# Recurrent branch, memory attention and pool product emitted one step behind every fifth dense product

## The chip, the cores and the metric

The kernel runs on one core of one Trainium2 chip. The metric is the device time of one execution in microseconds, the median of three runs. The engines are TensorE (PE in the profile, its weight loads PEld), VectorE (DVE), ScalarE (ACT), GpSimd (POOL) and SyncE (SP, which here issues the DMAs).

## The reference

One layer of a streaming encoder on 2048 tokens of width 1024, all float32, cut to what matters:

```python
h = rms_norm(x, norm_mix_g)
p = h @ w_in_mix                                  # 1792 rwkv + 256 pool + 256 memory query columns
y_a = rwkv7_branch(p_rwkv, ...)                   # 8 heads of 64, delta rule:
#   s_kk = S @ kk_t
#   S = S * w_t - outer(s_kk, kk_t * a_t) + outer(v_t, k_t);  y_t = S @ r_t
#   then group norm per head, bonus sum(r*k*r_k)*v, output gate
y_b = pool_branch(p_pool, pool_w, pool_scale)     # causal means over 2/4/8/16 tokens, 64x64 products
y_c = memory_branch(q_mem, rms_norm(mem), w_mem_kv)   # 4 heads, softmax over 256 memory tokens
gates = sigmoid(h @ w_gate + b_gate)              # three gates of 1024
merged = gates[0] * (y_a @ w_up_rwkv) + gates[1] * (y_b @ w_up_pool) + gates[2] * (y_c @ w_up_mem)
x = x + merged @ w_o
x = x + conv_ffn(rms_norm(x), ...)                # 1024 -> 2 x 2816 -> 1024, depthwise conv of 3, GELU
out = rms_norm(x, norm_final_g)
```

## The kernel before

**Tiling.** The mixers run over four tiles of 512 tokens (`for i in range(NT)`, L868); the FFN follows in two halves of 1024 tokens. Channels lie on the partitions, tokens on the free axis.

**Dense products.** Every dense product is made in three passes of high and low parts: for each 128 rows of the contraction three matmuls of 512 columns, hi x hi, hi x lo, lo x hi (`dense_fm`, L165 to L167; `dense_acc`, L173 to L175). A weight piece is 128 x 512 as hi and lo, 512 KB, and serves twelve matmuls in the mixers. In the first tile a piece is loaded as float32 and split (hi on ScalarE, L131, lo on GpSimd, L132), and the result is written to a cache in DRAM; the later tiles load the pieces from there (`wsp<-wc_...`). The pieces go through a ring of `WB` = 4 buffers.

**The recurrent branch** takes the eight heads in four pairs (b = 0 to 3). Of each pair, `rkv(b)` projects r, k and v. `rwkv()` is the preparation: the lora products (L452, L453), a head sum (`head_sum`, L302 and L303, two matmuls with a matrix of ones), a prefix scan, the scaled keys `E` (in `Z`) and `BK`, their products chunk by chunk (L510) under masks (L516 to L519), a bounce of the strictly triangular blocks through DRAM (`Ld` to `As`), and a forward substitution in 62 short VectorE operations (L539 and L541 in turn, "the solve"), whose result `X` goes through DRAM (`Xd`) into the block diagonal `TB`. `rwkv_chain()` then centres v (L562, L563), transposes BK into `BKt` (L572), joins the blocks of the inverse (`T`, L576; L580, L587) and goes through eight chunks of 64 tokens in sequence. A chunk step is three links, each a TensorE product and a short operation that the next one needs: L600, then `Rn` (L602 on VectorE, L603 on ScalarE); L607, then `UV` (L608, L609); L610, then the state `SV` (L615). After the eighth chunk come the outputs Y (L621, L624), the group norm and the output gate.

**Memory attention** (`mem_branch`) forms scores (L291 to L293), a softmax, its transposes (L423) and the product with the values; **pool** (`pool_branch`) forms running means on GpSimd and VectorE and one product (L385).

**Order.** A string of tokens, `SEQ`, gives the order in which a tile's blocks are written: `aN` the projections of pair N, `rN` its preparation, `cN` its whole chain, `pN` pool, `qN` and `mN` memory queries and attention, `gN` a block of gates 1 and 2 and `vN` the pool and memory up-projections, `kN` a block of gate 0, and `l x e s` loads and norm sums. After the string come the recurrent up-projection and w_o. The scheduler of the tile framework may move instructions against the written order when its model finds an operand late, so the chain's links end up between dense products.

## Time and profile before

| | us |
|---|---|
| Time, median of 3 runs (lowest to highest) | 3464.53 (3462.49 to 3466.19) |
| Profiled execution, its own time | 3465.13 |
| its span | 3463.3 |
| TensorE busy | 3278.9 |
| VectorE busy | 1884.8 |
| ScalarE busy | 1073.2 |
| GpSimd busy | 920.3 |

The profile is one execution. Its span goes from the first to the last record. TensorE's matmuls are pipelined, and the ends of their records are modelled. In the rows that give busy times for a stretch, the columns are: start and end of the stretch in us, its length, busy time of PE, PEld, DVE, ACT and POOL (with the number of instructions), the mean granted TensorE clock as a share of full speed, the busy share of the DMA engines and GB/s. In rows on waits they are total us, number of waits and the longest; in rows on groups of instructions busy us and mean ns, then idle time before them. A float32 matmul of the side branches has two records, or a count of two.

The tiles' first lora products stand at 67.4, 599.9, 1064.7 and 1527.8 us, and the FFN begins at 1973 us; these are the cuts between the stages. Tile 2 is also cut at the first L600 of each pair's chain (1136.0, 1227.7, 1283.8, 1356.6) and at its eighth (1181.0, 1266.3, 1319.1, 1390.2).

### The profile page before, as it was taken

What the parts mean: (1) busy time and instruction counts of PE and PEld (TensorE: products, weight loads), DVE (VectorE), ACT (ScalarE), POOL (GpSimd) and SP (SyncE); (2) the same over time, 40 slices, a digit from 0 to 9 for tenths busy, and PEclk for the clock granted to TensorE, in tenths of its full rate; (3) what the DMA queues carried; (4) which work ended last, traced back from release to release, by engine and by line L of the source; (5) the groups of instructions that cost most, each with busy time, mean ns of one, the idle gap of its engine ahead of it and who ended that gap; (6) DMA issues with size and microseconds to landing.
All of it is one profiled execution on the core that took longest, in us unless ns stands there. A gap on an engine that the chain in (4) does not pass through costs nothing.

```text
span 3463.3 us, 44769 instructions
## 1 busy us (share of the span) xinstructions
PE 3278.9 (95%) x16752; PEld 2588.4 (75%) x16752; DVE 1884.8 (54%) x3610; ACT 1073.2 (31%) x1999; POOL 920.3 (27%) x1094
## 2 busy tenths in 40 slices
PE   6988899989999999999999999999999999999998
PEld 4765677666787667876677788888888778888887
DVE  4788641888437885348872433443445554344435
ACT  4354343434213432224342221221222322122122
POOL 4254443122111222021220232322322342232223
PEclk8999999999999999999999999999999999999999
DMA  7444677344574345663445721111112141111111
GB/s 242 156 159 153 206 257 248 117 131 137 169 248 152 119 122 167 222 190 107 139 141 164 261 61 40 61 46 38 59 51 67 49 155 46 37 58 53 37 49 64
DMA packets 203274, 431.18 MB, mean 124 GB/s; under 512 B 54193, under 2 KB 66097, under 8 KB 202929
## 3 DMA queue, kind: packets, MB, share of 16 engines
q1 hardware_dynamic: 203056, 428.32, 38.7%
q8 instruction: 132, 2.16, 0.3%
q14 instruction: 86, 0.70, 0.1%
HBM read 346.44 MB, written 81.80 MB: 124 GB/s over the span
## 4 chain that ended last, share of the span: by engine, by line
PE 71%; DVE 17%; DMA 4%; issue 3%; ACT 3%; POOL 1%; SPq 0%; POOLq 0%; ACTq 0%; DVEq 0%
PE mm L722 9%; PE mm L724 9%; PE mm L723 9%; PE mm L167 7%; PE mm L166 7%; PE mm L165 7%; DVE xm L539 4%; PE ch L759 4%; PE ch L757 4%; PE ch L758 4%; DVE X L541 3%; PE mx L510 1%; PE ch L600 1%; PE ch L607 1%; PE ch L610 1%
## 5 line engine op out<-in xcount | busy, mean ns | idle before, releaser
L132 POOL TENSOR_TENSOR wsp<-wraw,wsp 128x512 fp32r<-128x512 f32 x380 | 507.9, 1344 | 1123.3 <-ACT wsp L131 1080.6
L165 PE MATMUL mm<-h,wsp 128*128 128x512 f32 x1344 | 554.1, 413 | 7.5 <-ACT h L226 2.6
L167 PE MATMUL mm<-h,wsp 128*128 128x512 f32 x1344 | 555.6, 413 | 4.1 <-POOL wsp L132 3.8
L166 PE MATMUL mm<-h,wsp 128*128 128x512 f32 x1344 | 552.5, 411 | 0.6 <-POOL h L226 0.5
L131 ACT CAST wsp<-wraw 128x512 fp32r<-128x512 f32 x380 | 230.5, 618 | 819.5 <-PE mm L724 498.5
L165 PEld LDWEIGHTS mm<-h,wsp 128*128 128x128 f32 x1344 | 261.3, 194 | 60.6 <-issue 5.4
L167 PEld LDWEIGHTS mm<-h,wsp 128*128 128x128 f32 x1344 | 261.2, 194 | 57.9 <-POOL wsp L132 6.8
L761 DVE TENSOR_TENSOR acc<-acc,ch 128x512 f32<-128x512 f32 x288 | 197.9, 688 | 190.7 <-PE ch L759 189.1
L166 PEld LDWEIGHTS mm<-h,wsp 128*128 128x128 f32 x1344 | 261.4, 195 | 53.3 <-issue 3.1
L722 PE MATMUL mm<-h2a,wsp 128*128 128x512 f32 x704 | 276.7, 393 | 0.0
L722 PE MATMUL mm<-h2b,wsp 128*128 128x512 f32 x704 | 275.9, 392 | 0.0
L724 PE MATMUL mm<-h2a,wsp 128*128 128x512 f32 x704 | 275.5, 391 | 0.0
L724 PE MATMUL mm<-h2b,wsp 128*128 128x512 f32 x704 | 275.2, 391 | 0.0
L723 PE MATMUL mm<-h2b,wsp 128*128 128x512 f32 x704 | 274.3, 390 | 0.0
L723 PE MATMUL mm<-h2a,wsp 128*128 128x512 f32 x704 | 274.2, 389 | 0.0
L736 DVE TENSOR_SCALAR tg<-U,cwu 128x512 f32<-128x512 f32 x88 | 74.0, 841 | 294.4 <-ACT U L733 294.3
L539 DVE TENSOR_TENSOR xm<-X,As 128x16 f32<-128x16 f32 (+30 forms) x496 | 224.8, 453 | 12.4
L757 PE MATMUL ch<-G,wsp 128*128 128x512 f32 x576 | 226.8, 394 | 2.4 <-DVE acc L761 2.4
L759 PE MATMUL ch<-G,wsp 128*128 128x512 f32 x576 | 227.7, 395 | 0.0
L758 PE MATMUL ch<-G,wsp 128*128 128x512 f32 x576 | 226.7, 394 | 0.0
L606 POOL TENSOR_SCALAR SV<-SV,dC 64x64 f32<-64x64 f32 x224 | 120.9, 540 | 333.1 <-DVE SV L615 202.6
L747 DVE TENSOR_TENSOR G<-tg,G 128x512 fp32r<-128x512 f32 x88 | 89.9, 1021 | 122.4 <-ACT G L746 122.4
(350 smaller groups left out, 5879.5 us busy)
## 6 DMA issues: line engine op xcount, KB each, us to landing
wsp<-wc_w_gate SPq DMA_DIRECT2D x144, 512.0 KB, 3.7
wsp<-wc_w_in_mix SPq DMA_DIRECT2D x108, 512.0 KB, 3.4
wraw<-in_w_ffn_in SPq DMA_DIRECT2D x176, 256.0 KB, 2.7
wc_w_gate<-wsp SPq DMA_DIRECT2D x48, 512.0 KB, 3.0
wsp<-wc_w_o SPq DMA_DIRECT2D x48, 512.0 KB, 4.9
wraw<-in_w_ffn_out SPq DMA_DIRECT2D x88, 256.0 KB, 2.7
wc_w_in_mix<-wsp SPq DMA_DIRECT2D x36, 512.0 KB, 2.9
wraw<-in_w_gate SPq DMA_DIRECT2D x48, 256.0 KB, 3.8
```

The costliest lines, as they stand in the source:

```text
L131: sc.copy(hi, raw[:, :n])
L132: gp.tensor_tensor(lo, raw[:, :n], hi.bitcast(F32), ALU.subtract)
L165: te.matmul(acc, hi, act(0, k), start=k == 0, stop=False)
L166: te.matmul(acc, hi, act(1, k), start=False, stop=False)
L167: te.matmul(acc, lo, act(0, k), start=False, stop=k == kn - 1)
L539: ve.tensor_tensor(xm[:, :, 0:t + 1], X[:, :, 0:t + 1], As[:, 0:t + 1, t].unsqueeze(1).to_broadcast([P, 8, t + 1]), ALU.mult)
L722: te.matmul(ab[t], ws[j][0], hk(0, t, k), start=k == 0, stop=False)
L723: te.matmul(ab[t], ws[j][0], hk(1, t, k), start=False, stop=False)
L724: te.matmul(ab[t], ws[j][1], hk(0, t, k), start=False, stop=k == KB - 1)
L757: te.matmul(a, ws[j][0][:, cs], G[:, j, 0, tk], start=j == 0, stop=False)
L758: te.matmul(a, ws[j][0][:, cs], G[:, j, 1, tk], start=False, stop=False)
L759: te.matmul(a, ws[j][1][:, cs], G[:, j, 0, tk], start=False, stop=j == 1)
```

## The change

The tokens `a`, `r`, `c` and the second `m` leave the order string, and the ring of weight pieces shrinks from four buffers to three. `rwkv`, `rwkv_chain`, `mem_branch` and `pool_branch` become generators that yield at set places (`wait(n)` yields n times). All dense matmuls of the mixers go through `dense_mm`, which counts them, and behind every fifth (`SPACING`) calls `run()`, which moves each branch under way on by one step: attention, pool, the preparation of one pair and the chain of another. What a step writes is tied behind that matmul, and the scheduler does not move it ahead. A chain begins at the earliest 33 steps (`SOLVE`) after its pair's preparation has been written. A preparation that wants buffers of an older chain yields until that has read them (`free`). At a few places the remaining steps are run out at once (`until`). The BK transposes move from the chain to the preparation, `BKt` gets a second buffer, the stores to `Ld` move ahead of the bonus head sum, and some temporaries change buffers.

```diff
-WB = 4
+WB = 3
+SPACING, SOLVE = 5, 33
-SEQ = "a0 l x r0 e p0 p1 q0 m0 q1 a1 m1 c0 r1 a2 g0 r2 g1 v0 g2 g3 v1 g4 c1 a3 g5 v2 g6 c2 r3 g7 s v3 g8 g9 v4 g10 g11 v5 g12 g13 c3 v6 g14 g15 v7 k0 k1 k2 k3 k4 k5 k6 k7".split()
+ORDER = "l x e q0 q1 m p0 p1 g0 g1 v0 g2 g3 v1 g4 g5 v2 g6 g7 s v3 g8 g9 v4 g10 g11 v5 g12 g13 v6 g14 g15 v7 k0 k1 k2 k3 k4 k5 k6 k7".split()
+    def dense_mm(*args, **kw):
+        mm = te.matmul(*args, **kw)
+        fill["n"] += 1
+        if fill["run"] is not None and fill["n"] >= SPACING:
+            fill["n"] = 0
+            with tc.issue_after(mm.ins):
+                fill["run"]()
...
-        qt = sb.tile([P, 2, TT], F32R, tag="x", name="qt", bufs=2)
+        qt = sb.tile([P, 2, TT], F32R, tag=("UV", "SV")[b], name="qt")
...
-                pr = scr[:, (2 + hh) * TT:(3 + hh) * TT]
+                pr = rt(("ys", "y2")[hh])
+            yield from wait(4)
+            for hh in range(2):
+                pr = prs[hh]
                 tp = bank("mx", 2)
...
-        ss = head_sum(sq, rt("kk", dt=F32R), rt("rn", dt=F32R))
+        sp = split_sum(sq, rt("kk", dt=F32R), rt("rn", dt=F32R))
+        yield from wait(3)
+        ss = head_sum(*sp)
...
+        early = 0
+        while not free(b):
+            early += 1
+            yield
...
+        BKt = sb.tile([P, 8, P], F32, tag="BKt", name="BKt", bufs=2)
+        yield from wait(9 - min(early, 4))
         for u in range(2):
+            yield
...
+        for u in range(2):
+            yield
+            kz = bank("mx", 2)
+            for c in range(4):
+                te.transpose(kz[:, c * P:(c + 1) * P], BK[:, 4 * u + c, :], ident)
+            sc.copy(BKt[:, 4 * u:4 * u + 4].rearrange("p c t -> p (c t)"), kz)
...
+        SV = sb.tile([P, 2, 8, C], F32, tag="SV", name="SV")
         UV = sb.tile([P, 2, 8, C], F32, tag="UV", name="UV")
...
         for c in range(8):
+            yield
             ch = bank("ch", 2)
...
+            yield
             te.matmul(ch[:, P:P + C], TB[:, c, :], Rn, start=True, stop=True)
...
+            yield
             te.matmul(ch[:, 2 * P:3 * P], BKt[:, c, :], UV[:, :, c, :], start=True, stop=True)
...
+        def run():
+            tick[0] += 1
+            for key in ("mem", "pool"):
+                if key in side:
+                    go(key)
+            b = at["prep"]
+            if "prep" not in side and b in parts and b <= at["values"] + 1:
+                side["prep"] = rwkv(i, b, *parts.pop(b), twd, sgd, ya, Z, free)
+            if "prep" in side:
+                ended, value = go("prep")
+                if ended:
+                    ready[b] = (tick[0], value)
+                    at["prep"] = b + 1
+            b = at["chain"]
+            if "chain" not in side and b in ready and (tick[0] >= ready[b][0] + SOLVE or keep.get("rush")):
+                side["chain"] = rwkv_chain(i, b, sgd, ya, at, *ready.pop(b)[1])
+                at["values"] = b + 1
+            if "chain" in side and go("chain")[0]:
+                at["chain"] = b + 1
```

In the new code all dense matmuls of the mixers stand on one line, L164; L639, L647 and L651 are the links that were L600, L607 and L610, and L580, L582 the solve's two operations.

On TensorE, in tile 2, a chunk step of the chain of pair 3, before:

```order
L600 MATMUL ch<-SV,Z 128x128
L165 MATMUL mm<-h,wsp 128x512
L166 MATMUL mm<-h,wsp 128x512
L167 MATMUL mm<-h,wsp 128x512
L607 MATMUL ch<-Rn,TBb 128x64
L165 MATMUL mm<-h,wsp 128x512
L166 MATMUL mm<-h,wsp 128x512
L167 MATMUL mm<-h,wsp 128x512
L610 MATMUL ch<-UV,BKt 128x128
```

Now there, on TensorE:

```order
L639 MATMUL ch<-SV,Z 128x128
L164 MATMUL mm<-h,wsp 128x512 x5
L647 MATMUL ch<-Rn,TBb 128x64
L164 MATMUL mm<-h,wsp 128x512 x5
L651 MATMUL ch<-UV,BKt 128x128
L164 MATMUL mm<-h,wsp 128x512 x5
```

Five dense matmuls stand between two links instead of three.

On VectorE, in tile 2, the third chunk step of pair 0's chain, before (`Z` and `BK` here are the preparation of pair 1):

```order
L602 TENSOR_SCALAR Rn<-ch 64x64
L492 SCALAR_TENSOR_TENSOR rta<-rta,rkk 128x512
L497 TENSOR_TENSOR Z<-rkk,rq 64x8x64
L608 COPY UV<-ch 64x64
L497 TENSOR_TENSOR Z<-rkk,rq 64x8x64
L498 SCALAR_TENSOR_TENSOR BK<-rta,rQ 64x8x64
L615 SCALAR_TENSOR_TENSOR SV<-ch,dC,SV 64x64 x2
```

Now there, on VectorE (`xm` and `X` are the solve of pair 1):

```order
L641 TENSOR_SCALAR Rn<-ch 64x64
L580 TENSOR_TENSOR xm<-X,As 128x8x14
L582 TENSOR_REDUCE X<-xm 128x8
L580 TENSOR_TENSOR xm<-X,As 128x8x15
L582 TENSOR_REDUCE X<-xm 128x8
L648 COPY UV<-ch 64x64
L580 TENSOR_TENSOR xm<-X,As 128x8x16
L582 TENSOR_REDUCE X<-xm 128x8
L580 TENSOR_TENSOR xm<-X,As 128x8x17
L582 TENSOR_REDUCE X<-xm 128x8
L656 SCALAR_TENSOR_TENSOR SV<-ch,dC,SV 64x64
```

The large operations of the next pair's preparation have moved ahead of this chain, and the solve's short pairs stand between its links.

On TensorE the end of pair 3's chain, now (L663 and L666 are Y, L316 and L317 the head sum of the group norm, L680 the output gate, `ya` the recurrent up-projection's input):

```order
L663 MATMUL ch<-Z,SV 64x64 x16
L666 MATMUL ch<-LP,UV 64x64 x16
L164 MATMUL mm<-h,wsp 128x512 x15
L316 MATMUL ch<-hl,one_r 128x512
L317 MATMUL ch<-hl,one_r 128x512
L680 MATMUL ch<-sgd,gl 128x512
L164 MATMUL mm<-h,wsp 128x512 x18
L164 MATMUL mm<-ya,wsp 128x512 x96
```

Between the chain's last link and the recurrent up-projection stand 33 dense matmuls and a few more inside the chain's last step; before, the chain ended among the gate 1 and 2 blocks and the whole of gate 0 stood between.

## Rows read from the trace of the kernel before

**Rows 1.** The head of the page: span, and each engine's busy time.

```profile
span 3463.3 us, 44769 instructions
PE 3278.9 (95%) x16752; PEld 2588.4 (75%) x16752; DVE 1884.8 (54%) x3610; ACT 1073.2 (31%) x1999; POOL 920.3 (27%) x1094
```

**Rows 2.** Busy times of stages: tile 0, tile 2, FFN.

```profile
core 0: us, PE busy (x) PEld busy (x) DVE busy (x) ACT busy (x) POOL busy (x), PEclk, DMA share, GB/s
...
67.40:599.90 532.50, 473.86 (x2580) 358.69 (x2581) 330.11 (x684) 219.96 (x422) 224.82 (x223) 0.93 0.60 197
...
1064.70:1527.80 463.10, 439.25 (x2550) 338.52 (x2549) 291.60 (x675) 161.07 (x316) 79.17 (x121) 0.97 0.53 162
...
1973.00:3463.00 1490.00, 1473.34 (x6498) 1208.39 (x6496) 655.29 (x869) 348.80 (x598) 433.86 (x473) 0.99 0.18 59
```

**Rows 3.** Busy times of 50 us of the FFN.

```profile
2000.00:2050.00 50.00, 50.00 (x220) 41.07 (x219) 18.32 (x23) 15.10 (x26) 19.31 (x23) 1.00 0.21 69
```

**Rows 4.** Busy times of the nine stretches of tile 2.

```profile
1064.70:1136.00 71.30, 64.40 (x339) 47.93 (x338) 64.43 (x151) 28.29 (x61) 11.48 (x18) 0.98 0.40 127
1136.00:1181.00 45.00, 42.86 (x271) 30.74 (x270) 34.32 (x74) 22.27 (x52) 11.47 (x20) 1.00 0.31 95
1181.00:1227.70 46.70, 40.64 (x267) 32.56 (x266) 43.12 (x99) 18.70 (x29) 9.29 (x8) 0.97 0.46 140
1227.70:1266.30 38.60, 37.46 (x231) 27.07 (x229) 30.50 (x93) 9.99 (x27) 8.53 (x19) 0.95 0.49 144
1266.30:1283.80 17.50, 17.38 (x154) 12.70 (x155) 13.06 (x30) 11.24 (x18) 2.46 (x4) 1.00 0.38 105
1283.80:1319.10 35.30, 32.95 (x227) 23.95 (x225) 28.37 (x62) 12.88 (x32) 12.61 (x16) 1.00 0.47 147
1319.10:1356.60 37.50, 32.50 (x226) 26.03 (x225) 28.38 (x77) 15.81 (x26) 4.86 (x6) 0.97 0.72 217
1356.60:1390.20 33.60, 33.46 (x192) 24.01 (x190) 8.88 (x32) 6.17 (x21) 7.83 (x14) 0.83 0.32 102
1390.20:1527.80 137.60, 137.60 (x658) 113.53 (x657) 40.55 (x61) 35.72 (x54) 10.64 (x16) 1.00 0.73 225
```

**Rows 5.** Waits of TensorE in tile 2.

```profile
PE mx L510 <- DVE BK L500: 7.7, 2, 5.1
PE ch L580 <- DVE T L576: 5.0, 1, 5.0
...
PE mx L423 <- DVE Z L420: 3.3, 1, 3.3
```

**Rows 6.** Groups of VectorE instructions in tile 2.

```profile
L539 DVE TENSOR_TENSOR xm<-X,As 128x16 f32<-128x16 f32 (+30 forms) x124 | 52.9, 427 | 3.1
L541 DVE TENSOR_REDUCE X<-xm 128x8 f32<-128x16 f32 (+30 forms) x124 | 36.4, 293 | 2.8
```

**Rows 7.** TensorE in order of time in pair 3's chain: start, duration, instruction.

```profile
1369.33 0.43 PE L607 MATMUL ch<-Rn,TBb 128*128 128x64 f32 x2
...
1370.12 0.40 PE L166 MATMUL mm<-h,wsp 128*128 128x512 f32 x1
1370.35 0.39 PE L167 MATMUL mm<-h,wsp 128*128 128x512 f32 x1
...
1372.45 0.46 PE L600 MATMUL ch<-SV,Z 128*128 128x128 f32 x2
...
1373.53 0.43 PE L607 MATMUL ch<-Rn,TBb 128*128 128x64 f32 x2
```

**Rows 8.** DMA issues in tile 2: count, size, median us from issue to landing.

```profile
wsp<-wc_w_gate SPq DMA_DIRECT2D x48, 512.0 KB, 3.7
wsp<-wc_w_in_mix SPq DMA_DIRECT2D x36, 512.0 KB, 3.7
wsp<-wc_w_o SPq DMA_DIRECT2D x16, 512.0 KB, 4.7
```

**Rows 9.** A wait of SP's DMA queue in tile 2.

```profile
SPq L84 <- DVE X L541: 12.5, 3, 7.9
```

More of the change, by code (lines that the diff above doesn't have):

```diff
@@ L361, in p_shift, with wait, pool_branch @@
         return o
-    def pool_branch(i, h, ybc, j, scr):
-        acc = dense_fm("w_in_mix", 14 + j, h, KB)
+    def wait(n):
+        for _ in range(n):
+            yield
+    def pool_branch(i, acc, ybc, j, scr):
         W = TT + 15
@@ L425, in mem_branch @@
                 split(pv[0], pv[1], tp.rearrange("p (t m n) -> p t m n", t=2, m=2))
+            yield from wait(3 if qp else 1)
         o = bank("mx", 2)
@@ L955, in block_kernel @@
             elif k == "p":
-                pool_branch(i, h, ybc_(), n, scr)
+                acc = dense_fm("w_in_mix", 14 + n, h, KB)
+                until(lambda: "pool" not in side)
+                side["pool"] = pool_branch(i, acc, ybc_(), n, scr)
+                go("pool")
+                keep["scr"] = n == 1
             elif k == "q":
```

110 lines of the change are left out of this document (70 added, 40 removed).

## The prediction

> **What bounds the kernel now.** I read the page's busy line first, then the busy times stage by stage, then one steady token tile cut at its own sync points, then what TensorE waits for there. TensorE is busy 95% of the 3463.3 us span [rows 1], but by stage that share says little [rows 2]: the FFN (from 1973 us) has it busy 1473.3 of 1490 us, a token tile 439.25 of 463.1. A stretch of dense products alone issues 220 matmuls in 50 us, 0.2275 us each [rows 3], although in the order of time a dense matmul is shown busy for 0.40 us with the next one's start 0.23 us later [rows 7]: records of neighbours overlap, so a stretch can look busy and still issue below its rate. So I price TensorE by counts. A tile has 1392 dense matmuls (eighteen in_mix blocks and 24 gate blocks of 24, eight up blocks of pool and memory and eight of the recurrent branch at 12, eight w_o blocks of 24): 1392 x 0.2275 = 316.7 us. The side matmuls (recurrent branch, attention, pool) are not in those rows; from start to start they take about 75.6 us a tile, an estimate from the shorter distances to the next record of each line (0.2 to 0.3 us for those of a chain link). As a bound above, the stretch at 1266.3 us has 31 dense and 69 side matmuls in 17.5 us without an idle gap [rows 4]: (17.5 - 7.1)/69 = 0.15 us each, 100 us for all 666. So a tile could take 392 us (at most 417) and takes 463.1: some 70 us are stalls or slow issue. The FFN and the stage ahead of the tiles keep their code; of the change only the smaller weight ring reaches the FFN, and there a piece serves 24 matmuls (5.46 us), so two pieces of cover are 10.9 us.
>
> Where the 70 us lie shows when tile 2 is cut at its first lora product and at the first and last chunk step of each pair's chain [rows 4]. By counts of the instruction order TensorE needs, in the nine stretches, 57.7, 35.9, 36.6, 30.8, 14.1, 27.6, 29.8, 24.4 and 135.5 us; they take 71.3, 45.0, 46.7, 38.6, 17.5, 35.3, 37.5, 33.6 and 137.6. In the first seven VectorE is busy 64.4, 34.3, 43.1, 30.5, 13.1, 28.4 and 28.4 us, in three of them longer than TensorE's need and in the others within 1.6 us of it, so that two queues of like length wait for each other in turn. A third of VectorE's time is the forward-substitution solve (52.9 + 36.4 = 89.3 us a tile in 248 short operations [rows 6]). Then pair 3's chain runs with VectorE nearly idle (8.9 of 33.6 us) and a mean granted clock of 0.83, that is part of the time at the lower of TensorE's two levels (1.2 instead of 2.4 GHz), which follows waits in the stretch before. Last comes a tail of 137.6 us in which TensorE has 574 dense matmuls and VectorE 40.6 us of work. So dense products stand idle as cover: too few of them where VectorE works, and 130.6 us where it does not.
>
> **The change part by part.** (1) *Instructions.* Nothing is added to any engine's arithmetic: 3610 VectorE instructions, the same matmuls. TensorE's price stays 392 us a tile; only stalls can change.
>
> (2) *Where the dense products lie.* One step of each running side branch now follows every fifth dense matmul. Counted in the new order, the nine stretches hold 270, 107, 63, 110, 80, 106, 89, 105 and 462 dense matmuls instead of 179, 89, 132, 106, 31, 87, 109, 85 and 574. So 112 matmuls, 25.5 us, leave the tail and cover the front. With the side matmuls TensorE needs 89.0, 30.5, 22.3, 29.8, 27.7, 29.4, 25.5, 28.0, 110.0; VectorE (its operations dealt out by its new order at their mean durations in this tile) 92.6, 35.7, 21.2, 31.0, 25.6, 27.2, 10.0, 6.4, 41.9. I sum four kinds.
> First stretch, lora to chain 0: 71.3 before, 6.9 above VectorE's busy time. Now the larger queue is VectorE with 92.6 (attention's softmax and part of the pool work move in); with the same 7, 100.
> Four chains: 45.0 + 38.6 + 35.3 + 33.6 = 152.5 before. Taking for every link the larger of the two queues gives 42.6, 37.2, 34.4 in the old order for pairs 0 to 2, within 2.4 us of the trace, so I trust it: 41.2, 37.9, 36.6 in the new one. VectorE still stands with two solve pairs (2 x (0.427 + 0.293) = 1.44 us [rows 6]) between the links, against 5 x 0.2275 = 1.14 us of dense work on TensorE, so little goes there. Pair 3 has no solve beside it; it had 3 to 5 dense matmuls between links (one chunk step takes 4.20 us, its closest link 1.08 [rows 7]). Five are 1.14 us, above 1.08, so TensorE should not wait: 28.1. Sum 144.
> Three stretches between chains: 46.7 + 17.5 + 37.5 = 101.7 before, 14.7 above the larger queue of each (43.1, 14.1, 29.8). The single waits there include the inverse's half product on its transpose, 5.0 us [rows 5], now a step of its own behind five dense matmuls. New larger queues 22.3, 27.7, 25.5 = 75.5; with 8.5 left of the excess, 84.
> Tail: 137.6 before, 2.1 above TensorE's price; now 110.0, and 4 because the last pair's group norm has 15 and 18 dense matmuls as cover in place of a whole gate phase: 114.
> Sum 100 + 144 + 84 + 114 = 442, against 463.1: 21 us a tile.
>
> (3) *Waits that end.* The mask products on BK and the transposes on the softmax cost 7.7 and 3.3 us in tile 2 [rows 5]; both now have steps of dense work ahead. They and the slow clock after them are inside the sums of (2) and not counted again.
>
> (4) *Moved work.* The BK transposes go from chain to preparation (16 matmuls, eight to a step, two ACT copies); a second BKt buffer pays for it. The Ld bounce is issued before the bonus head-sum. On SP the four Ld stores only move up. I cost both at nothing, covered by the 33 steps (33 x 1.14 = 38 us) held between preparation and chain; without that cover a landing like those of [rows 8], some 5 us, would show for each pair, 20 a tile. The queries move into buffers of the chain and the probabilities into those of its group norm; by TensorE's order the last attention product stands some 90 dense matmuls (20 us) before chain 0's first chunk step, so the chain does not wait for them.
>
> (5) *Weight ring of three instead of four.* A piece serves 12 matmuls, 2.73 us. Three buffers hide a load that lands within 2 x 2.73 = 5.46 us of its issue, four within 8.2. The rows: 3.7 us median for gate and in_mix, 4.7 for w_o [rows 8]. SP is held by the solve's last result 12.5 us in three times, at most 7.9 [rows 9]; with one buffer less each such hold can cost up to 2.73 us more, some 8 us a tile where nothing else runs, but it falls in stretches where VectorE is the longer queue. Cost taken 0, bound 8 a tile.
>
> Four tiles. Tile 3 has the same order up to the FFN. Tile 0 takes 532.5 us [rows 2] because weights are split on ScalarE and GpSimd as they come (224.8 us of GpSimd); its stalls are partly of that kind, so I take the same 21 there, give or take 20. Sum 4 x 21 = 84. The profiled execution took 3465.13 us, 0.6 above the median of the runs, with 1.8 outside its span: 3465.1 - 84 = **3381 us**.
>
> One rule of the Trainium skill speaks on how much room there is. By TensorE's busy time a steady tile idles 463.1 - 439.25 = 23.9 us, so no order could gain more than 24 a tile (3465 - 96 = 3369). The Trainium skill (Trainium Kernel Development and Optimization, Performance Expectations) says that matmul busy time is a bad measure of the distance to roofline since matmuls are pipelined, and that the share of weight loading is a good one. By the loads a tile is at 338.5/463.1 = 73% where the FFN is at 1208.4/1490 = 81% [rows 2]; brought to the FFN's share a tile takes 417 us, 46 less. By that rule the trace agrees with it: 220 matmuls in 50 us would be 88 us of busy records.
>
> **Rivals.** *More:* stalls nearly vanish, tiles reach the 417 us at which weight loads have the FFN's share: 4 x 46 = 184, 3281 us. For it: the price by counts is lower still; the larger queues alone sum to 403. Against: VectorE and TensorE are within 5 us of each other in five stretches, and two in-order queues so close rarely overlap fully. Chance 0.13.
> *Less:* the front becomes a serial path. Lora, head-sum, mask products and softmax transposes now stand behind 3 to 9 steps of 1.14 us each, and VectorE has no other ready work. If the first stretch takes 107 (89.0 and 18 of such waits), the chains 150 and those between 86, a tile takes 457, 6 less: 3441 us. For it: VectorE fills 92.6 of the front already. Chance 0.20.
> *Slower:* the ring. In the tail the pieces are asked for at full rate with the DMA engines 73% busy at 225 GB/s [rows 4]. If loads there land after 7.9 us (the longest hold of SP), every piece costs (7.9 - 5.46)/3 = 0.81 us more: 38.5 pieces give 31 a tile, 10 more than is gained, 3506 us. It decides from a landing of 5.46 + 3 x 21/38.5 = 7.1 us. Against: medians of 3.7 and 4.7 in the same rows. Chance 0.08.
> That the change does not do what it says is excluded by the order: five matmuls between links stand there.
>
> **How the numbers follow.** Forecast 0.59, with its own range from 10 to 33 us a tile and 20 either way in tile 0: about 3320 to 3430. More 0.13 (3225 to 3330), of which 0.08 lies under 3320; less 0.20 (3425 to 3465), of which 0.04 lies above 3455; slower 0.08. The range 3320 to 3455 leaves out 0.20. A difference under 0.2% (7 us) can't be told from none by these runs. Faster 0.59 + 0.13 + 0.16 = 0.88; same 0.03; slower 0.08 and 0.01 of "less" = 0.09.
>
> **What would show it.** Right: tiles of about 442 us, the clock at 0.97 or above in pair 3's chain, which then takes 28 to 30 us, a tail of about 114, a first stretch near 100 with VectorE busy over 90, and the waits on BK, T and the softmax gone. Wrong: a first stretch above 105, new TensorE waits on VectorE at chain links in pairs 0 to 2 of more than 10 us a tile, or waits on weight loads in the tail.

## The result and the profile after

The changed kernel takes 3425.18 us (median of four runs, 3424.09 to 3431.77); the kernel before took 3465.36 beside it. The ratio is 0.9889, with an interval of 0.9872 to 0.9907: 40 us faster, clear of the noise, where 84 had been forecast.

The head of the page of the changed kernel:

```profile
span 3424.4 us, 44585 instructions
PE 3251.7 (95%) x16752; PEld 2568.3 (75%) x16752; DVE 1872.8 (55%) x3610; ACT 1072.7 (31%) x1993; POOL 924.4 (27%) x1094
```

TensorE has the same 95% as in [rows 1]; again this share tells nothing. To see where the 40 us came from I cut both traces at every 1392nd dense matmul, that is tile by tile (columns as in [rows 2]). Before:

```profile
17.00:570.90 553.90, 480.99 (x2604) 361.08 (x2605) 343.30 (x701) 233.22 (x445) 242.18 (x237) 0.93 0.61 201
570.90:1035.70 464.80, 439.32 (x2548) 337.84 (x2549) 290.50 (x674) 160.67 (x315) 77.89 (x121) 0.98 0.52 163
1035.70:1498.90 463.20, 439.35 (x2550) 338.60 (x2550) 291.61 (x675) 161.07 (x316) 79.17 (x121) 0.97 0.52 162
1498.90:1973.20 474.30, 444.04 (x2549) 340.90 (x2548) 301.01 (x684) 161.92 (x314) 81.47 (x122) 0.97 0.52 162
```

And after:

```profile
17.00:561.80 544.80, 469.59 (x2604) 352.66 (x2604) 342.73 (x701) 234.13 (x445) 245.41 (x236) 0.95 0.61 204
561.80:1018.50 456.70, 434.79 (x2549) 334.06 (x2549) 287.28 (x675) 159.49 (x315) 79.32 (x121) 0.98 0.52 165
1018.50:1478.90 460.40, 435.66 (x2548) 335.15 (x2549) 286.53 (x674) 159.73 (x314) 79.81 (x121) 0.98 0.50 162
1478.90:1935.10 456.20, 436.31 (x2550) 335.64 (x2549) 296.49 (x684) 160.26 (x311) 80.65 (x121) 0.98 0.54 171
```

The tiles win 9, 8, 3 and 18 us, where 21 each had been forecast; the FFN takes 1489 us and wins nothing. One execution fixes a single tile only to some 4 us: a second one of the changed kernel (a_again below) has 545, 459, 457 and 454 us. Now the nine stretches of tile 2, cut as in [rows 4] at the first lora product and at the first and last chunk step of each chain:

```profile
1048.90:1161.10 112.20, 103.53 (x572) 76.92 (x571) 88.89 (x193) 44.82 (x93) 14.10 (x21) 0.95 0.38 121
1161.10:1197.20 36.10, 34.33 (x156) 24.36 (x154) 33.46 (x104) 12.04 (x28) 11.28 (x19) 1.00 0.42 137
1197.20:1225.70 28.50, 27.39 (x269) 21.13 (x269) 21.54 (x36) 16.12 (x27) 7.17 (x7) 0.94 0.36 113
1225.70:1261.60 35.90, 33.58 (x161) 24.95 (x160) 29.72 (x97) 13.77 (x33) 9.71 (x19) 1.00 0.62 205
1261.60:1298.80 37.20, 33.59 (x289) 25.29 (x290) 27.05 (x44) 16.29 (x29) 8.51 (x9) 0.91 0.38 116
1298.80:1333.30 34.50, 32.57 (x159) 24.68 (x157) 26.74 (x89) 6.92 (x20) 8.22 (x14) 1.00 0.54 172
1333.30:1361.70 28.40, 28.11 (x260) 22.05 (x260) 11.73 (x25) 11.46 (x19) 3.71 (x6) 1.00 0.54 166
1361.70:1391.10 29.40, 29.32 (x148) 24.27 (x147) 7.01 (x28) 5.74 (x18) 5.32 (x12) 1.00 0.48 161
1391.10:1509.30 118.20, 113.25 (x546) 91.45 (x545) 41.08 (x63) 32.74 (x49) 11.82 (x17) 1.00 0.69 221
```

By the forecast's four kinds: the first stretch takes 112 (forecast 100), the four chains 36.1 + 35.9 + 34.5 + 29.4 = 136 (144), the three stretches between them 28.5 + 37.2 + 28.4 = 94 (84), the tail 118 (114). The chains did better, all else worse; the sum is 460 instead of 442. The clock of pair 3's chain is 1.00 instead of 0.83, as forecast. TensorE's waits in this tile (total us, times, longest):

```profile
PE mx L543 <- DVE Z L551: 5.5, 3, 2.8
PE ch L639 <- DVE SV L656: 4.0, 10, 0.7
PE mx L543 <- DVE BK L531: 2.6, 1, 2.6
PE mm L164 <- DMA wsp<-wc_w_o: 2.5, 2, 1.5
PE mx L446 <- DVE rys L440: 2.4, 1, 2.4
PE ch L625 <- ACT T L621: 1.7, 1, 1.7
PE mm L164 <- DMA wsp<-wc_w_up_rwkv: 1.2, 1, 1.2
```

The masks and BK (L510 in [rows 5], here L543) and the softmax transposes (L423, here L446) are still waited for, 10.5 us together against 11.0 and 0.8 more on Z; the wait at the inverse is down from 5.0 to 1.7; waits on weight loads in the tail are new in this tile with 3.7 (tile 3 had 3.0 before and has 3.2). All waits of TensorE in tile 2 together, summed from its records, are 24 us before and 25 after.

One part of the gain can be bounded from the granted clock. The mean over the span, before, after, and in the best version below:

```profile
core 0: 3463.3 us, clock 0.975
```

```profile
core 0: 3424.4 us, clock 0.980
```

```profile
core 0: 3396.9 us, clock 0.986
```

Span times (1 - clock) is the most that the lower level can have cost: 87, 68 and 48 us. A quarter of the time at the lower level finds TensorE with nothing running, where the clock costs nothing; without it 65, 52 and 37 us are lost. So some 13 of the 40 us, at most 18, are a clock that fell less often. The executions of the kernel before agree: over the 55 on record 0.01 of mean clock goes with 26 us, and the clock rose by 0.005.

The rest can be summed from the distances between the starts of TensorE's records. Over the four tiles (1956 us before, 1918 after) its waits fall from 153 to 142 us, the loss at the lower clock from 61 to 48, and the side products' own distances, with what the lower level adds taken off, from 381 to 344; the dense products take 23 us more than 0.2275 each than they did (95 before, 118 after). The second execution of the changed kernel has 142, 45, 344 and 117.

### The profile page after: what moved, and what is told of

Read it like the earlier page. It is cut to its first block, busy times and chain, and to the rows that moved or that the text cites. A ratio compares the mean times of both kernels' runs of the same rounds, so it can differ in the third digit from the quotient of the medians.

```text
span 3424.4 us, 44585 instructions
## 1 busy us (share of the span) xinstructions
PE 3251.7 (95%) x16752; PEld 2568.3 (75%) x16752; DVE 1872.8 (55%) x3610; ACT 1072.7 (31%) x1993; POOL 924.4 (27%) x1094
## 4 chain that ended last, share of the span: by engine, by line
PE 72%; DVE 17%; DMA 4%; issue 3%; ACT 2%; POOL 1%; SPq 0%; POOLq 0%; ACTq 0%; DVEq 0%
PE mm L164 23%; PE mm L767 9%; PE mm L769 9%; PE mm L768 9%; DVE xm L580 5%; PE ch L804 4%; PE ch L803 4%; PE ch L802 4%; DVE X L582 3%; PE mx L543 1%; DMA wsp<-wc_w_o 1%; DVE SV L656 1%; POOL wsp L133 1%; DVE BK L529 1%; PE mm L802 1%
## 5 line engine op out<-in xcount | busy, mean ns | idle before, releaser
L164 PE MATMUL mm<-h,wsp 128*128 128x512 f32 x4032 | 1102.0, 413 | 10.4 <-ACT h L238 3.0
L164 PEld LDWEIGHTS mm<-h,wsp 128*128 128x128 f32 x4032 | 734.4, 192 | 169.2 <-issue 13.8
L781 DVE TENSOR_SCALAR tg<-U,cwu 128x512 f32<-128x512 f32 x88 | 84.7, 963 | 383.7 <-ACT U L778 383.6
L580 DVE TENSOR_TENSOR xm<-X,As 128x16 f32<-128x16 f32 (+30 forms) x496 | 231.6, 467 | 9.1
L769 PEld LDWEIGHTS mm<-h2a,wsp 128*128 128x128 f32 x704 | 132.1, 188 | 30.1
L769 PEld LDWEIGHTS mm<-h2b,wsp 128*128 128x128 f32 x704 | 132.1, 188 | 29.5
L768 PEld LDWEIGHTS mm<-h2a,wsp 128*128 128x128 f32 x704 | 132.2, 188 | 29.3
L768 PEld LDWEIGHTS mm<-h2b,wsp 128*128 128x128 f32 x704 | 132.2, 188 | 28.5
L767 PEld LDWEIGHTS mm<-h2b,wsp 128*128 128x128 f32 x704 | 132.2, 188 | 27.9
```

The costliest lines, as they stand in the source:

```text
L164: mm = te.matmul(*args, **kw)
L580: ve.tensor_tensor(xm[:, :, 0:t + 1], X[:, :, 0:t + 1], As[:, 0:t + 1, t].unsqueeze(1).to_broadcast([P, 8, t + 1]), ALU.mult)
L767: te.matmul(ab[t], ws[j][0], hk(0, t, k), start=k == 0, stop=False)
L768: te.matmul(ab[t], ws[j][0], hk(1, t, k), start=False, stop=False)
L769: te.matmul(ab[t], ws[j][1], hk(0, t, k), start=False, stop=k == KB - 1)
```

## Experiments

Two theories stood against each other at first. The *VectorE theory* is the prediction's: in the first stretch and in the chains of pairs 0 to 2 VectorE is the longer queue. The *TensorE theory*: these stretches are TensorE's own issue, dearer than I had priced it, plus waits.

**What fills the first stretch and the chains.** a_halfsolve leaves out every second step of the forward substitution:

```diff
-        for t in range(1, 32):
+        for t in range(1, 32, 2):
```

> The changed kernel with every second step of the forward substitution left out: 16 of the 31 pairs of operations for each pair of heads remain, some 10.8 us of VectorE less for each pair, 43 a tile. VectorE theory (the prediction's): VectorE is the longer queue in the first stretch (112 us in tile 2) and in the chains of pairs 0 to 2; the first stretch falls by 8 or more and the three chains (36, 36, 34) to about 30 each, 25 us a tile, about 3325. TensorE theory: the first stretch is TensorE's own 95 us of issue and 17 of waits for operations ahead of the solve; it stays at 110 or above, only the waits of the chain links on SV go (4 to 7 us a tile), about 3400.

Measured 3393 us (ratio 0.9797, 0.9765 to 0.9828). The first stretch of tile 2 and the chains of pairs 0 to 2:

```profile
1033.90:1139.90 106.00, 101.77 (x573) 75.52 (x573) 79.17 (x163) 44.83 (x94) 14.07 (x21) 0.97 0.42 129
1139.90:1174.90 35.00, 33.20 (x156) 24.31 (x155) 26.74 (x77) 11.06 (x28) 8.90 (x19) 1.00 0.46 147
...
1203.50:1239.80 36.30, 32.08 (x158) 24.34 (x156) 22.35 (x70) 12.93 (x31) 8.94 (x18) 1.00 0.66 202
1277.80:1311.60 33.80, 32.19 (x160) 24.72 (x159) 22.37 (x69) 6.87 (x20) 8.49 (x14) 1.00 0.58 183
```

VectorE has 7 and 7 us less to do in the first two chains and they take 35.0 and 36.3 instead of 36.1 and 35.9. The VectorE theory wanted chains of 30 and 100 us in all; 32 came, 13 of them in tile 0. VectorE does not set the chains. The first stretch falls by 6 in this tile, part of it at the clock; over tiles 1 to 3 it is 106 us on average, against 110 in two executions of the changed kernel, for 10 us less of VectorE. That is less than the 8 of the VectorE theory, and more than the TensorE theory allowed: VectorE has some part in the first stretch.

a_mem1 takes work from TensorE alone, the attention's passes with low parts:

```diff
+    def mm1(out, a, b, start=True, stop=True):
+        te.matmul(out, a[0], b[0], start=start, stop=stop)
...
-                    mm3(sb2[hh][:, t * NMEM:(t + 1) * NMEM], ...)
+                    mm1(sb2[hh][:, t * NMEM:(t + 1) * NMEM], ...)
-                mm3(o[:rows], ...)
+                mm1(o[:rows], ...)
```

> The changed kernel with one pass instead of three in the attention's two products (the passes with the low parts are left out): 48 of 72 matmuls fewer a tile, on TensorE alone; in tile 2 the three lines take 11.6 us from start to start. TensorE theory: the first stretch, in which they all lie, is TensorE's own issue and falls from 112 by nearly what they take, 7 to 8 us, about 30 us in all, 3395. VectorE theory: VectorE's work there is unchanged, the first stretch stays within 2 us, 3425.

Measured 3410 us (0.9843, 0.9799 to 0.9887). The first stretch of tile 2:

```profile
1046.50:1149.90 103.40, 96.20 (x472) 71.39 (x471) 88.05 (x194) 44.07 (x90) 13.55 (x21) 0.97 0.40 124
```

VectorE is as busy as before (88), and the stretch is 8.8 us shorter, in tiles 1 and 3 by 5 and 7: it follows TensorE's work more than VectorE's. The run does not tell issue from the attention's own path, which is shorter by the same products. About half of the gain is given back in the stretches after it, so the total falls by 15 and not by 30, and its interval overlaps that of the changed kernel.

**What a side product costs.** In the trace a dense matmul that follows a short float32 product is slow. From the kernel before, pair 3's chain, in order of time (start, duration):

```profile
1369.57 0.47 PE L167 MATMUL mm<-h,wsp 128*128 128x512 f32 x1
1369.88 0.40 PE L165 MATMUL mm<-h,wsp 128*128 128x512 f32 x1
```

The one behind L607 holds TensorE from 1369.57 to 1369.88, 0.31 us, the next one 0.24 [rows 7]. My price of a side product had been its own distance to the next start, and this first dense product had not been counted with it. a_dum1 and a_dum8 measured the thing by itself, on the dense products of the recurrent up-projection and w_o, with the same 48 transposes a tile:

```diff
         mm = te.matmul(*args, **kw)
         fill["n"] += 1
+        if fill.get("tail") is not None:
+            fill["t"] += 1
+            if fill["t"] % 6 == 0:            # a_dum8: % 48
+                with tc.issue_after(mm.ins):
+                    for _ in range(1):        # a_dum8: range(8)
+                        te.transpose(fill["tail"][:, 0:P], ident, ident)
...
```

> The changed kernel with one more float32 transpose of the identity (its result is not used) behind every sixth dense product of the recurrent up-projection and w_o, 48 a tile, where nothing else runs beside the dense products. Theory of the switch: in the trace the first dense product after a short float32 side product takes 0.315 us to the next start instead of 0.2275, on top of the side product's own 0.11 to 0.14; then each costs 0.20 to 0.23 us, 10 to 11 us a tile, 40 to 44 us in all, near 3467. Rival: a side product costs its own slot alone, 0.11 to 0.14 each, 21 to 27 us, near 3450.

> The same 48 transposes a tile in six groups of eight behind every 48th of these dense products. Theory of the switch: 48 times 0.11 and six times 0.09, 5.8 us a tile, 23 us in all, near 3449, some 15 us below the run in which they stand singly, with the same matmuls. Rival (own slots alone): the two runs agree within 4 us.

Measured 3438 us (0.9914, 0.9885 to 0.9943) and 3431 (0.9897, 0.9864 to 0.9930), some 9 and 3 us above the changed kernel by the ratios, instead of 42 and 23; all three intervals overlap, so the price must be read from the traces. Two consecutive ones of a_dum1 in the tail:

```profile
1418.46 0.27 PE L171 MATMUL ch<-ident 128*128 128x128 f32 x1
1419.96 0.27 PE L171 MATMUL ch<-ident 128*128 128x128 f32 x1
```

Six dense products and one transpose take 1.50 us; less 6 x 0.2275 that is 0.13 for one. Its own distance to the next start is 0.03 (median), and the dense product behind it takes 0.09 more. In groups of eight a transpose takes 0.10, or 0.11 with its share of the dense product behind the group. So my expectation had counted the own slot twice, and a step that stands alone costs little more than one in a group: *that* theory, a dear switch, fell. What stays is that own distance and the slower neighbour belong together. Besides, the tails grew by only 2 us in tiles 1 and 2 for 6 us of added work: the rest went into time in which the tail waited anyway (TensorE's waits on weight loads in tile 2's tail are 0.9 us there, 3.7 in the changed kernel).

**The weight ring.** b_ring3 is the ring's part of the change alone:

```diff
-WB = 4
+WB = 3
```

> The kernel before with one edit: three weight buffers instead of four. Ring theory: in the changed kernel the tail of tile 2 loses 6 us to weight loads that had not landed (0.2 before), and the ring of three is the cause; then the kernel before loses about as much in each tail, and the same again where SP is held, 5 to 8 us a tile, 3485 to 3497 us. Rival: those waits come from the loads standing at other places of SP's queue in the new order; then the ring of three alone costs nothing, 3465 within 7.

Measured 3467 us beside 3462 (1.0018, 1.0002 to 1.0034): 6 us, where the ring theory wanted 20 to 30 and its rival none. In its trace the cost is in tile 3 (487 us instead of 474), where TensorE waits 12.9 us for weight loads instead of 3.0; tiles 1 and 2 are no slower.

a_ring4 gives the changed kernel the fourth buffer back, at the price of a raw buffer:

```diff
-WB = 3
+WB = 4
...
-        raw = sb.tile([P, 512], F32, tag="wraw", name="wraw", bufs=3)
+        raw = sb.tile([P, 512], F32, tag="wraw", name="wraw", bufs=2)
...
-        lraw = sb.tile([P, 2 * P], F32, tag="lraw", name="lraw")
+        lraw = sb.tile([P, 2 * P], F32, tag="T11", name="lraw")
```

> The changed kernel with four weight buffers (room is made by two instead of three buffers for raw weights and by putting the raw lora weights into T11's buffer). Ring theory: the tail of tile 2 goes from 118 to 112 us, matmul-to-matmul excess there under 1 us, all in all 20 to 25 us less, about 3402. Rival (place in SP's queue): tail stays at 118, 3425 within 7. Tile 0 and the FFN may lose a little by the smaller raw ring and are read apart.

Measured 3464 us (1.0003, 0.9988 to 1.0018), all the gain gone. Tile 0, and the two largest of its waits:

```profile
17.00:605.60 588.60, 493.10 (x2605) 364.42 (x2606) 342.62 (x700) 231.98 (x442) 242.34 (x236) 0.93 0.55 189
```

```profile
PE mm L164 <- ACT wsp L132: 35.3, 19, 3.4
PE ch L639 <- DVE SV L656: 14.7, 14, 1.7
```

Tile 0 takes 588.6 instead of 544.8 us: with two raw buffers TensorE waits 35 us for the splitting of weights. Tiles 1 to 3, which split none, take 453.4, 457.5 and 453.3, some 3 us less each than 456.7, 460.4 and 456.2, but no less than a_again's 459, 457 and 454 in two of the three. a_raw4 went the other way:

```diff
-        raw = sb.tile([P, 512], F32, tag="wraw", name="wraw", bufs=3)
+        raw = sb.tile([P, 512], F32, tag="wraw", name="wraw", bufs=4)
...
-        lraw = sb.tile([P, 2 * P], F32, tag="lraw", name="lraw")
+        lraw = sb.tile([P, 2 * P], F32, tag="T11", name="lraw")
```

> The changed kernel with four raw weight buffers instead of three (the raw lora weights lie in T11's buffer). In the run with two, tile 0 took 588.6 instead of 544.8 us. If tile 0 waits for raw loads because ScalarE and GpSimd give the raw buffers back late, the fourth gives back part of it: tile 0 at 520 to 535, tiles 1 to 3 as they are, 3400 to 3415. Rival: three buffers are enough and the loss with two was a threshold: 3425 within 6.

Measured 3433 us (0.9917, 0.9885 to 0.9949), not faster; tile 0 takes 557 us in its trace. A fourth gives nothing here, though both runs also put the raw lora weights into T11's buffer, whose own cost no run separates. To read the ring cleanly, a_r4 has four weight and three raw buffers, beside a_again, the changed kernel unedited on the same chip:

```diff
-WB = 3
+WB = 4
...
-        lraw = sb.tile([P, 2 * P], F32, tag="lraw", name="lraw")
+        lraw = sb.tile([P, 2 * P], F32, tag="raw", name="lraw", bufs=2)
...
-        gl = sb.tile([P, P], F32, tag="gl", name="gl", bufs=2)     # preparation
...
-            xm = sb.tile([P, 8, 32], F32, tag="xm", name="xm")
+            xm = sb.tile([P, 8, 32], F32, tag="T11", name="xm")
...
+        gl = sb.tile([P, P], F32, tag="gl", name="gl")             # chain's start
...
-            Rn = sb.tile([P, C], F32, tag="Rn", name="Rn", bufs=2)
+            Rn = sb.tile([P, C], F32, tag="Rn", name="Rn")
```

> The changed kernel again, beside its variants on one chip: ratio 0.987 to 0.991 to the kernel before.

> The changed kernel with four weight buffers and, unlike the run in which the raw weights had two, all three raw buffers (room: the solve's product and the raw lora weights share other buffers, the output gate's weights are loaded at the chain's start into one buffer, Rn has one). Ring theory: the tail of a tile (118 us against 110 of TensorE's own) loses its weight waits; with two raw buffers tiles 1 to 3 were 3 us faster each. Then 3 to 7 us for each tile: 3398 to 3413. Rival: four buffers give nothing as in the kernel before, 3425 within 6.

Measured 3427 us (0.9899, 0.9877 to 0.9921) for a_again, a repeat of the result, and 3427 (0.9906, 0.9881 to 0.9932) for a_r4. The tails of tiles 1 to 3 are 1 to 4 us shorter, the first stretches 1 to 3 longer. The ring of three costs the change nothing that these runs can tell; whether the smaller buffers that pay for the fourth lengthen the first stretches was not tested.

**The spacing.** a_sp6 and a_sp4 change one number, a_sp6s18 two:

```diff
-SPACING, SOLVE = 5, 33
+SPACING, SOLVE = 6, 33
```

> The changed kernel with a step behind every sixth dense product. TensorE theory: a wait of TensorE goes when it has a sixth product before the next step; first stretch's waits (11 us in tile 2) halve and the links' waits (2.5 us a chain) go, with the slow clock that follows them: 10 to 15 us a tile less, 3365 to 3385, the first stretch longer (about 120) and the tail shorter (about 75). VectorE theory: the first stretch and chains 0 to 2 are set by VectorE and do not grow with the dense products put into them, 112 and 36, so the whole 37 us that leaves the tail is won, 3300 or less. Rival: the steps that no longer fit are run out at once ahead of the recurrent up-projection, whose waits eat the gain: 3425 within 10, with waits of 10 us or more in the last chain.

Measured 3559 us (1.0273, 1.0249 to 1.0298), 134 slower than with five. The rival had the place right and the size wrong: the last chain no longer fits ahead of the recurrent up-projection and runs out at once. In order of time, late in pair 3's chain of tile 2 (in brackets the wait ahead and for what), and the last half of that chain's stretch:

```profile
1471.49 0.46 PE L639 MATMUL ch<-SV,Z 128*128 128x128 f32 x2
...
1474.90 0.77 PE L639 MATMUL ch<-SV,Z 128*128 128x128 f32 x2 [0.85 <-DVE SV L656]
...
1477.52 0.80 PE L651 MATMUL ch<-UV,BKt 128*128 128x128 f32 x2 [0.55 <-ACT UV L649]
1479.17 0.77 PE L639 MATMUL ch<-SV,Z 128*128 128x128 f32 x2 [0.85 <-DVE SV L656]
1480.56 0.69 PE L647 MATMUL ch<-Rn,TBb 128*128 128x64 f32 x2 [0.62 <-ACT Rn L642]
1481.79 0.80 PE L651 MATMUL ch<-UV,BKt 128*128 128x128 f32 x2 [0.55 <-ACT UV L649]
```

```profile
1477.50:1491.70 14.20, 7.55 (x20) 5.01 (x20) 3.44 (x14) 1.28 (x6) 2.65 (x6) 0.50 0.00 0
```

The first chunk step without any dense product takes 3.41 us from link to link (1471.49 to 1474.90), all but the last 0.7 at the full clock; then the clock has fallen, and at its lower level (0.50) a bare step takes 4.27. With fifteen dense products in it, after the change, a step takes 29.4/7 = 4.20 at the full clock. So fifteen dense products, 3.4 us of work, make a step 0.8 us longer than the first bare one, and no longer than the bare ones behind it. Beside this the projections of pair 1 came 60 products later, because they may only start between two pairs of gate blocks; the stretch ahead of pair 1's chain took 56 us instead of 28.

a_sp6s18 tried to make room by a smaller distance between preparation and chain:

```diff
-SPACING, SOLVE = 5, 33
+SPACING, SOLVE = 6, 18
```

> The changed kernel with a step behind every sixth product and 18 instead of 33 steps between preparation and chain, so that the chains nearly fit (in the order, only the last pair's end stands among the recurrent up-projection's products). With six products between links a link (1.36 us without cover) is covered by 1.37 + 0.24 us. If the waits at links and in the front cost what the rows show (link waits about 7 us a tile, front 8 and 5 at the lower clock), tiles fall by 8 to 15 us: 3365 to 3395. Rival: with 18 steps (108 products, 25 us) the solve's result is not there and TensorE waits for it ahead of each pair's L617, 5 to 10 us a pair: slower than 3440.

Measured 3490 us (1.0077, 1.0047 to 1.0107). TensorE waits for the inverse (5.2 us in tile 2), as the rival said, but the same slip of pair 1's projections cost more: 57 us ahead of its chain. A single wait for a gate weight piece takes 6.8 us besides.

a_sp4:

```diff
-SPACING, SOLVE = 5, 33
+SPACING, SOLVE = 4, 33
```

> The changed kernel with a step behind every fourth dense product. Without cover a link takes 1.36 us (28.5 us for seven chunk steps in a run in which the last chain stood alone). Four products with the switch take 1.02 us and the link 0.14, 1.16: TensorE waits 0.2 us at each of 96 links, 19 us a tile, and more in the front: 3490 to 3520, the seven chunk steps of pair 3 at 28.5. VectorE theory of the prediction: the stretches in which VectorE is longer do not change, and the tail grows by what leaves pair 3's chain: 3440.

Measured 3460 us (0.9986, 0.9969 to 1.0003): the change's gain is lost. The first stretch, the chains of pairs 0 and 3, and the tail, in tile 2:

```profile
1065.90:1156.50 90.60, 83.62 (x417) 61.47 (x415) 79.26 (x180) 40.85 (x85) 13.29 (x20) 0.96 0.38 120
1156.50:1197.70 41.20, 40.01 (x240) 28.71 (x240) 28.47 (x87) 8.65 (x25) 8.23 (x15) 0.88 0.34 106
...
1369.70:1394.90 25.20, 25.20 (x127) 19.53 (x125) 8.30 (x30) 5.58 (x19) 6.54 (x13) 1.00 0.43 136
1394.90:1526.60 131.70, 129.88 (x623) 106.26 (x623) 41.38 (x63) 34.58 (x52) 11.46 (x17) 1.00 0.73 225
```

My number for a link without cover, 1.36 us, was wrong, since the chain that it came from had run its second half at the lower clock: with four products pair 3's chain takes 25.2/21 = 1.20 us a link and does not wait. Nor is the loss in this tile: the mask products of pair 1 now fall into pair 0's chain (41.2 instead of 36.1 us) and the tail is 13 us longer, with 78 more dense products in it, but the first stretch is shorter by 22, and the tile takes 460.7 us as against 460.4. Tiles 0, 1 and 3 lose 11, 6 and 20. Over the four tiles TensorE's waits are no longer than with five products (138 us against 142); the side products' own distances, taken in the same way, are back from 344 to 371, and the loss at the lower clock rises from 48 to 75.

**The distance of the masks.** a_waits puts three more steps ahead of the mask products and of the softmax transposes:

```diff
-        yield from wait(9 - min(early, 4))
+        yield from wait(12 - min(early, 4))
...
-            yield from wait(4)
+            yield from wait(7)
```

> The changed kernel with three more steps (15 dense products) ahead of the mask products and ahead of the softmax transposes. If TensorE's waits there (5.4 on the masks and BK, 2.7 on the softmax in tile 2's first stretch, and about 5 us lost at the lower clock behind them) come from too few products before the step, they go: 8 to 13 us a tile, 3375 to 3395, no half-clock stretch left in the first stretch. Rival: VectorE's queue in the front is a serial path and the wait only moves behind the new place: 3425 within 8, waits on the same tiles as before.

Measured 3488 us (1.0077, 1.0055 to 1.0098). The waits aimed at went (neither is among the twelve largest of tile 2; the largest is now one of 7.4 us for a gate weight piece), but in the order the last steps of the attention now stand together ahead of the first up-projection, run out without cover, and pair 1's projections slip by 60 products, as with six: 67.7 us between the chains of pairs 0 and 1.

```profile
1081.90:1173.20 91.30, 87.81 (x436) 63.84 (x434) 73.73 (x169) 35.41 (x78) 11.14 (x19) 0.98 0.39 123
...
1208.90:1276.60 67.70, 60.35 (x414) 47.90 (x414) 54.40 (x117) 29.96 (x50) 11.33 (x15) 0.95 0.51 169
```

a_mask2 moves two steps instead of adding any, so that every chain stands at the same dense products as in the changed kernel:

```diff
-        yield from wait(9 - min(early, 4))
+        yield from wait(11 - min(early, 4))
...
-        yield from wait(2)
         bs = head_sum(*sp)
```

> The changed kernel with two more steps (ten dense products) ahead of the mask products and two fewer ahead of the bonus head sum, so that the chains stand at the same dense products as before this edit. The waits of TensorE on the masks and on BK (5.4 us in tile 2's first stretch) and the slow clock behind them (6.8 us at half speed there) go if they come from too little distance: 5 to 8 us a tile, 3395 to 3405. Rival: VectorE is late by more than 2.5 us and the waits stay, or move to the next step: 3425 within 7.

Measured 3409 us (0.9836, 0.9810 to 0.9862), 16 to 18 less than the changed kernel. The stretches ahead of the chains of pairs 1 and 2, and these chains, in tile 2:

```profile
1186.00:1211.80 25.80, 24.11 (x252) 18.51 (x252) 18.57 (x33) 17.26 (x28) 7.06 (x7) 1.00 0.40 122
1211.80:1249.30 37.50, 35.49 (x180) 27.20 (x179) 30.72 (x97) 14.61 (x34) 9.87 (x19) 1.00 0.62 200
1249.30:1282.30 33.00, 30.39 (x272) 22.89 (x272) 25.14 (x43) 16.99 (x29) 7.85 (x8) 0.96 0.44 135
1282.30:1319.50 37.20, 35.38 (x176) 26.14 (x175) 29.29 (x90) 6.22 (x19) 8.26 (x14) 0.99 0.50 155
```

The place was another than I had thought. The first stretch keeps most of its waits (7.2 of 8.7 us), and its length (109.4) is that of a_again (109.7). The two stretches ahead of the chains take 25.8 and 33.0 instead of 28.5 and 37.2, at a clock of 1.00 and 0.96 instead of 0.94 and 0.91; but side products have moved from them into the chains, which take 37.5 and 37.2 instead of 35.9 and 34.5, so only 2.6 of these 6.9 us are left. Over the four tiles TensorE's waits fall from 142 to 134 us and its loss at the lower clock from 48 to 37 (45 in a_again): the gain is the clock's as much as the waits'.

**One part alone, and the best version.** b_bkt is the kernel before with the ring of three, the second BKt buffer and the moved transposes, and no side work:

```diff
-WB = 4
+WB = 3
...
+        BKt = sb.tile([P, 8, P], F32, tag="BKt", name="BKt", bufs=2)   # after the bonus, in rwkv
+        for u in range(2):
+            kz = bank("mx", 2)
+            for c in range(4):
+                te.transpose(kz[:, c * P:(c + 1) * P], BK[:, 4 * u + c, :], ident)
+            sc.copy(BKt[:, 4 * u:4 * u + 4].rearrange("p c t -> p (c t)"), kz)
...
```

> The kernel before with one part of the change alone: three weight buffers, BKt with two buffers, and the BK transposes at the end of the preparation instead of at the chain's start. If the gain comes from the spacing of the steps, this gives none: 3460 to 3475. Rival: TensorE's wait at the chain's start (the transposes behind the copies of SV, 14.8 us in tile 0) was a good part of the loss: 3445 or less.

Measured 3457 us (0.9983, 0.9965 to 1.0000): 6 us, between 0 and 12. The remaining 28 to 40 come, by elimination, from the spacing and the new places; the two were not taken apart.

a_best has a_mask2's and a_r4's edits:

> Both edits that helped: the mask products two steps later, and four weight buffers with three raw buffers. If the two waits are separate, their gains add: 16 us and 12 to 28 us below the changed kernel, 3381 to 3398. Rival: the weight waits gone from the tail show up as waits in the front, about 3408.

Measured 3398 us (0.9821, 0.9800 to 0.9842), faster than both kernels. The clock is 0.986. Against a_mask2 the gain is 11 us by the medians and 5 by the ratios, whose intervals overlap; that the ring adds something here is not shown.

## Why the prediction was half right

*Right:* the direction, and the places that gain. Pair 3's chain has no slow clock any more and takes 29.4 us (28.1 forecast). The tail falls by 19.4 us (23.6). The moved transposes and the ring give little or nothing (b_bkt, b_ring3), which leaves the spacing and the new places. Tile 0 kept its stalls.

*The step that failed is the price of TensorE's own work*, 392 us a tile, 75.6 of it for side products, and with it "only stalls can change". In the trace of before, with all start-to-start distances of the side records of tile 2 summed, they take 95.8 us, not 75.6: I had taken the shorter four fifths of each line and left out the rest as stalls. The dense product behind each of some 140 side groups takes 0.09 us more, 12 us, and I had booked that as stall too. So TensorE's own need is 316.7 + 95.8 + 12 = 425 us and the stalls are 39 of 463, not 70. After the change it is 316.7 + 88.8 + 13 = 419 of 460, that is 42 us of stalls. (Both sums carry what the lower clock adds inside side groups.) The 20 us of stalls that the forecast took away a tile are not gone at all in this tile: the waits that ended came back elsewhere (24 us before, 25 after). Over all four tiles the waits fell by 11 us and the loss at the lower clock by 13.

Nor was the price fixed. The side products' own time fell by 7 us in this tile, mostly at the chain links, whose own distance went from 0.24 to 0.18 us (0.14 in pair 3, where nothing waits). This is delay too short to show as a wait: in tiles 1 to 3 a link whose weight load follows the load before it within 0.1 us stands 0.14 to 0.16 us from the next start, one whose load comes later 0.21 to 0.22, alike before, after and in a_sp4; on time were 47 of 214 links before, 118 of 264 after and 62 of 223 with four products (links directly behind a dense product). The bound that I had worked out from the stretch at 1266.3 us, at most 417 us a tile, was nearer than 392, but the 425 lie above it too.

*The second failure follows from it.* With TensorE priced too low, VectorE looked like the longer queue in the first stretch and in three chains, and I added a small excess to VectorE's 92.6 us. a_halfsolve and a_mem1 show the reverse for the chains, and for the first stretch that TensorE's work weighs more than VectorE's (7 us for 7 to 8 of TensorE's work, 3 for 10 of VectorE's, on average over tiles 1 to 3). In the first stretch TensorE has 61.4 us of dense and 33.9 of side products (27.6 priced), and waits and a clock of 0.95 on top: 112. In the stretches between chains side products take 30.6 us where I had 22.7: 94 instead of 84. The chains, on the other hand, came out too long: in pair 0's chain TensorE needs 24.3 us for 107 dense products, 6.2 for side products and 2 for the dense ones behind them, 32.5 of the 36.1 that it takes; half of the solve taken away (a_halfsolve) gave 1 us of the rest. VectorE's 35.7 us of priced work run beside that and not in turn with it.

*Third:* stalls do not vanish when they are moved. L543 and L446 still wait 10.5 us in tile 2; I had let them go because steps of dense work stood ahead. a_mask2 shows that in the first stretch two steps more don't help, and that over the whole mixers they save some 8 us of waits. The tail of tile 2 has 3.7 us of weight waits that it did not have; I had put 0 for them, with 8 as a bound. A first stretch above 105 and weight waits in the tail were two of the three signs of being wrong that I had named.

*Of the rivals,* "less" (3441) came nearer to the result than the forecast, 16 us off against 44, and was right in part: the waits on the masks, BK and the softmax that it put into the first stretch stayed. Its sizes were not: TensorE's need there is 95 and not 89, the chains take 136 and not 150. "Slower" by the ring has little support: b_ring3 loses 6 us, and four buffers change nothing in a_r4. By the share of weight loading tile 2 stands at 335/460 = 73% as before, so the room that "more" counted on is still there. Against TensorE's need the loads are 335/419 = 80%, close to the FFN's 81%. (The rule of the Trainium skill, Trainium Kernel Development and Optimization, Performance Expectations, that the prediction weighed says that matmul busy time is a bad measure of the distance to roofline and the share of weight loading a good one. This trace agrees: busy records fill 436 us where the need is 419, and the 46 us of room by the share are near the 42 of stalls. It does not say how much of the room a change will get: the best version got 12 in this tile.)

Tile 3, whose time before (474 us) was 10 longer than that of tile 2, won its 18 us in two halves: 10 of waits (30 to 19 us, the wait at the inverse from 7.4 to 1.7) and 10 of the side products' own time.

*What stays open:* why a_mem1's gain in the first stretch was half given back (in tile 2 pair 0's chain took 38.8 instead of 36.1 us, at a mean clock of 0.91 instead of 1.00); and which of the new places, beside the spacing, the gain needs.

## What to carry to other kernels

Price the engine that everything is hidden under by distances between starts summed over *all* its records, not by the quiet ones; whatever the quiet ones leave out is not yet a stall, and not yet a fixed price either. Before moving cover to an engine that looks longer, take work from that engine alone and look whether anything gets shorter. In an order that is paced by counting, a change of one wait can shift a whole stage by a block (60 products here): compare the places of all later steps, and move waits in pairs so that these stay.

## What the runs showed of the hardware

A chunk step of three dependent links takes 3.41 us without any dense matmul in it at the full clock (a_sp6, but for its last 0.7 us), 25.2/7 = 3.60 with twelve (a_sp4), 4.20 with fifteen (after), and 4.27 without any once the clock has fallen to 0.50 (a_sp6).

A single float32 transpose between dense matmuls costs 0.12 to 0.13 us (a_dum1), of which only 0.03 stands at its own record and 0.09 at the dense matmul behind it; behind the head sums of 512 columns (L317, after) that matmul takes 0.23 and nothing is lost.

The lower clock took at most 87 of 3463 us in a kernel whose TensorE was shown busy for 95% of the span, and at most 48 of 3397 in the best version; without the time in which TensorE had nothing running it is 65 and 37, 28 of the 66 us between them.

When a chain link's weight load came late, the link stood 0.21 to 0.22 us from the next start instead of 0.14 to 0.16, with no wait shown (before, after, a_sp4).
